# Stick-breaking heads with later ticks: running sums at tick 20, turned weights split at 38 and used at 41, gate turned at 8

## The chip, the cores and the metric

The kernel runs on one core of a Trainium2 chip. A core has TensorE (PE in the profile; its weight loads are listed apart, as PEld), VectorE (DVE), ScalarE (ACT), GpSimd (POOL) and SyncE (SP), which here only issues transfers. Each engine takes its instructions in the order in which the program issues them, and waits on semaphores for what the others make. The metric is the device time of one execution in microseconds (us), lower is better; the profile comes from one execution, recorded by the hardware profiler.

## What is computed

Two layers of a decoder trunk over 256 positions of width 2048, everything in float32, then a final RMSNorm. Layer 0 has sparse attention and dilated attention; layer 1 has eight stick-breaking heads (mixer C) and eight forgetting heads (mixer D). Each layer is a norm, one input projection whose columns are the heads' queries, keys, values and gates, the heads, a gate, and an output projection that is added to the stream. The change is in mixer C. For one block of 128 queries:

```python
z = jnp.einsum('bqhd,bshd->bhqs', qb, k).astype(F32) * (HEAD_DIM ** -0.5)
before = (key_pos[None, :] < qpos[:, None])[None, None]
log_1m = jnp.where(before, jax.nn.log_sigmoid(-z), 0.0)
tail = lax.cumsum(log_1m, axis=3, reverse=True) - log_1m
w = jnp.where(before, jnp.exp(jax.nn.log_sigmoid(z) + tail), 0.0)
return jnp.einsum('bhqs,bshd->bqhd', w.astype(v.dtype), v)
```

and behind the heads `x + (y * jax.nn.silu(gate)) @ w_out`. The kernel forms softplus(z) as relu(z) + log(1 + exp(-|z|)), sums it from the right with a scan, and takes the weight as exp(z - sum).

## The kernel before

**Chunks and k steps.** The columns of each input projection are cut into chunks, one per head: for a stick-breaking head 512 columns, queries, keys, values and gate of that head. Head 1 is the exception: its queries and keys stand in chunk F1 with the forget gates (264 columns), its values and gate in chunk G1 (256). `project` (line 328) multiplies a chunk in 16 k steps of 128 rows. In each step, for each half of the 256 positions, three matmuls are added in PSUM: high part of the activations by high part of the weights, low by high, and high by low (lines 323, 324, 326). So a k step of a full chunk is six matmuls of 512 columns.

**Splitting the weights.** A transfer brings four k steps of weights (1024 KB, tile `raw`, three buffers). `split` (line 267) makes the two parts of two k steps at a time, which I call a half: ScalarE copies to `whi` (line 282), VectorE subtracts to `wlo` (line 283), four buffers each. A chunk has eight halves, 0 to 7. Before the k steps of a half are issued, the halves up to three further on are split (line 360, `AHEAD`), so that the split of half 3 of a chunk is the first that is issued after the chunk has begun.

**Ticks.** The heads are Python generators. After each k step of a full chunk `tick` (line 307) advances a clock by one, and every generator whose count has run out goes on: it issues its next instructions on all engines, and with `yield n` stands back for n ticks. So the order of the work on every engine is written by hand, in ticks; 16 ticks make a full chunk, 8 each make F1 and G1. A head starts (its tick 0) when its own chunk has been projected, while the next chunk is multiplied. Where several generators are due at one tick, the one that was started first goes first.

**One stick-breaking head** (`head_c`, line 933; `head_cf` for head 1). Ticks are from its own start.

- 0: `scaled_qk` (line 840) scales queries and keys out of PSUM (ScalarE line 845, VectorE line 846), `grid` (line 420) turns their 32 x 32 blocks on VectorE (line 428), and `vg1` (line 849) makes values and gate: exponential (line 856), reciprocal (861), product (866), parts of the values (484, 487). This is the head's opening work.
- 2 and 6: the turned blocks of queries and keys are stored to DRAM and read back in another order, which completes the transposition (`moved`, line 431). Both transfers are issued by SP, which waits in order for each.
- 4, 6 and 10: the gate `u` goes the same way (`gate_turned`, line 494): blocks turned, stored, read into `uT`.
- 10: `qk_parts` (line 403) cuts queries and keys into parts (lines 408 to 410).
- 14: `scores` (line 514) on TensorE; VectorE adds the mask (line 915); ScalarE forms softplus and relu (lines 918 to 921).
- 16: VectorE makes the running sums (two scans, line 924) and the difference (line 926), ScalarE the exponential (line 927). Tick 16 falls at the end of the next head's chunk, just ahead of that head's tick 0.
- 18, 20 and 24: the weights `z` are turned in blocks (line 428), stored, and read back by four transfers (line 442).
- 28: `weights_out` (line 546) cuts the turned weights into parts `ph` and `pl` and a copy `p1`.
- 31: `weigh_out` (line 505) multiplies values by weights on TensorE (lines 461 to 463 and 510, tile `o`), VectorE multiplies by the gate (line 511), and the product is cut into its place for the output projection.

Head 0 reads its queries and keys at tick 8 and forms its values in three ticks, with the later stages at the same places. The forgetting heads (`head_d`) have the same opening work and a softmax in place of lines 915 to 927; their gate still goes by `gate_turned`.

**Buffers.** `z` shares two buffers with the softmax tiles, `uT` has two, `v` has two and a third place for heads 2, 5 and the first forgetting head; `ph`, `pl`, `p1` and `sp` have one each. `far`, into which `grid` turns, has two, and the DRAM tiles four.

Of the kernel before, what the change touches and what calls it, by code (L numbers as in the profile page):

```python
# [7 lines left out]
F32 = mybir.dt.float32  # L8
# [6 lines left out]
P = 128  # L15
NT = 2
SEQ = 256
# [157 lines left out]
def trunk(ctx, tc, x, xT, g1, w0, wo0, w1, wo1, bf, gf, consts, rope, out):  # L175
    nc = tc.nc
    cp = ctx.enter_context(tc.tile_pool(name="cp", bufs=1))
    wp = ctx.enter_context(tc.tile_pool(name="wp", bufs=3))
    hp = ctx.enter_context(tc.tile_pool(name="hp", bufs=2))
    dr = ctx.enter_context(tc.tile_pool(name="dr", bufs=1, space=bass.MemoryType.DRAM))  # L180
# [112 lines left out]
    def start(g):  # L293
        n = next(g, None)
        if n is not None:
            side.append([g, n])
# [116 lines left out]
    def quarters(a):  # L413
        return a.rearrange("p (b i c) -> p b i c", i=4, c=32)

    def arrived(t, n):

        return t.rearrange("p (i b c) -> p b i c", i=4, b=n)

    def grid(srcs):  # L420

        t = hp.tile([P, 512], F32, name="far", tag="rt2")
        ns = [x.shape[1] // P for x in srcs]
        n = sum(ns)
        o = t[:, 0:P * n].rearrange("p (j b c) -> p b j c", j=4, b=n)
        for i, x in enumerate(srcs):
            b = sum(ns[:i])
            nc.vector.transpose(o[:, b:b + ns[i]], x.rearrange("p (b j l) -> p b j l", j=4, l=32))  # L428
        return t[:, 0:P * n]

    def moved(t, dst, done, stored, ordered=False):


        n = t.shape[1] // P
        d = dr.tile([P, P * n], F32, name="fard", tag=f"fard{n}", bufs=4)
        yield done
        nc.sync.dma_start(d, t)
        yield stored
        if ordered:
            w = P * n // 4  # L440
            for j in range(4):
                nc.sync.dma_start(dst[32 * j:32 * j + 32].rearrange("p (i f) -> p i f", i=4),
                                  d[:, j * w:(j + 1) * w].rearrange("(i l) f -> l i f", i=4))
            return
        nc.sync.dma_start(dst.rearrange("p (i f) -> p i f", i=4),
                          d.rearrange("r (j f) -> (r j) f", j=4).rearrange("(i q) f -> q i f", i=4))

    def far(srcs, dst, first, done, stored):

        yield first  # L450
        yield from moved(grid(srcs), dst, done, stored)

    def qk_turned(qk, ticks, last):

        yield last or ticks
        r = qk_parts(quarters(turn([qk[:, i * P:(i + 1) * P] for i in range(4)])) if last else arrived(qk, 4))
        yield 6 - last if last else 4
        return qk_of(r)

    def three_of(o, ah, al, bh, bl, first, last):  # L460
        nc.tensor.matmul(o, ah, bh, start=first, stop=False)
        nc.tensor.matmul(o, ah, bl, start=False, stop=False)
        nc.tensor.matmul(o, al, bh, start=False, stop=last)
# [8 lines left out]
    def cut(dst, src):  # L472

        nc.scalar.activation(dst[0], src, AF.Copy)  # L474
        nc.vector.tensor_tensor(dst[1], src, dst[0].bitcast(F32), op=OP.subtract)  # L475
# [18 lines left out]
    def gate_turned(u, n=NT):  # L494
        uT = hp.tile([P, P * n], F32, name="uT", tag="uT" if n == NT else "rl")
        start(far([u], uT, 4, 2, 4))
        return arrived(uT, n)

    def gate_turned_here(u):
        pt = turn([u[:, 0:P], u[:, P:SEQ]])  # L500
        uT = hp.tile([P, SEQ], F32, name="uT", tag="uT")
        nc.scalar.activation(uT, pt[:, 0:SEQ], AF.Copy)
        return quarters(uT)

    def weigh_out(ph, pl, p1, v, uT, kt):

        vh, vl, v1 = v
        po = pa.tile([P, SEQ], F32, name="o", tag="o", bufs=1)
        three_of(po, vh, vl, ph, pl, True, False)
        nc.tensor.matmul(po[:, P:SEQ], v1, p1, start=False, stop=True)  # L510
        nc.vector.tensor_tensor(uT, quarters(po), uT, op=OP.mult)  # L511
        cut([quarters(t[:, kt, :]) for t in ys], uT)

    def scores(qk):
        q0, k0, q1h, q1l, kh, kl = qk
        pS = pa.tile([P, 384], F32, name="s", tag="s", bufs=1)
        nc.tensor.matmul(pS[:, 0:P], q0, k0, start=True, stop=True)  # L517
        three(pS[:, P:384], q1h, q1l, kh, kl)
        return pS
# [26 lines left out]
    def weights_out(blocks, v, uT, kt, last):  # L546

        ph = hp.tile([P, SEQ], F32R, name="ph", tag="ph", bufs=1)
        pl = hp.tile([P, SEQ], F32R, name="pl", tag="pl", bufs=1)
        p1 = hp.tile([P, P], F32, name="p1", tag="p1", bufs=1)  # L550
        cut((quarters(ph), quarters(pl)), blocks[:, 0:2])
        nc.scalar.activation(quarters(p1), blocks[:, 2:3], AF.Copy)
        if last:
            uT = gate_turned_here(u=uT)
        yield 2 if last else 3
        weigh_out(ph, pl, p1, v, uT, kt)

    def softmax_head(qk, ticks, nb, v, u, rs, kt, last, near):

        uT = u if last else gate_turned(u)  # L560
        qk = yield from qk_turned(qk, ticks, last)
        pr, l = soft(qk, nb() if callable(nb) else nb)
        if not last:
            yield 2
        share(pr, factor(l, rs))
        if near:
            yield 4
            blocks = quarters(turn([pr[:, 0:P], pr[:, P:SEQ], pr[:, SEQ:384]]))
        else:
            yield from moved(grid([pr]), pr, 2, 4, True)  # L570
            yield 4
            blocks = arrived(pr, 3)
        yield from weights_out(blocks, v, uT, kt, last)
# [165 lines left out]
    def heads_a(ps, h):  # L739
# [7 lines left out]
        for th in (1, 0):  # L747
            nc.vector.scalar_tensor_tensor(u[:, :, th, :], tgs[th].rearrange("p (a b) -> p a b", a=2), 1.0,
                                           ps[th][:, 256:512].rearrange("p (a b) -> p a b", a=2),
                                           op0=OP.add, op1=OP.mult)  # L750
        uT = gate_turned(u.rearrange("p a b c -> p (a b c)"), 4)
        yield from far([qk], qk, 2, 2, 4)
        yield 4
# [154 lines left out]

    def stick(qk, ticks, v, u, kt):

        uT = gate_turned(u)
        qk = yield from qk_turned(qk, ticks, 0)
        pZ = scores(qk)
        z = hp.tile([P, 384], F32, name="z", tag="sn")
        nc.vector.tensor_tensor(z, pZ, smask, op=OP.add)
        sp = hp.tile([P, 384], F32, name="sp", tag="sp", bufs=1)
        zp = hp.tile([P, 384], F32, name="zp", tag="ih", bufs=1)
        nc.scalar.activation(sp, z, AF.Abs)
        nc.scalar.activation(sp, sp, AF.Exp, scale=-1.0)
        nc.scalar.activation(sp, sp, AF.Ln, bias=1.0)  # L920
        nc.scalar.activation(zp, z, AF.Relu)
        yield 2
        for _, s in BLK:
            nc.vector.tensor_tensor_scan(sp[:, s][:, ::-1], sp[:, s][:, ::-1], zp[:, s][:, ::-1], 0.0,  # L924
                                         op0=OP.add, op1=OP.add)
        nc.vector.tensor_tensor(z, z, sp, op=OP.subtract)
        nc.scalar.activation(z, z, AF.Exp)
        yield 2
        yield from moved(grid([z]), z, 2, 4, True)
        yield 4  # L930
        yield from weights_out(arrived(z, 3), v, uT, kt, 0)

    def head_c(ps, h):
        qk = scaled_qk(ps, 0, (0, 3), (1, 2))
        start(moved(grid([qk]), qk, 2, 4))
        v, u = yield from vg1(ps, 256, h == 0, h % 3 == 2)
        yield from stick(qk, 10 if h else 8, v, u, h)

    def head_cf(ps, qk):
        v, u = yield from vg1(ps, 0)  # L940
        yield from stick(qk, 10, v, u, 1)
# [133 lines left out]
```

## Time and profile before

| | |
|---|---|
| median of 3 runs | 915.04 us (914.64 to 915.21) |
| the profiled execution | 914.97 us |
| its span, first to last instruction | 913.2 us |
| mean granted TensorE clock | 0.993 |
| PE busy | 888.4 us, 97% of the span |
| DVE busy | 656.5 us, 72% |
| ACT busy | 477.2 us, 52% |
| DMA | 203.65 MB, mean 223 GB/s |

The span is what lies between the first and the last instruction; the execution's time has 1.8 us more. Busy is the time in which an engine has an instruction at work; matmuls are pipelined, so that a busy PE need not be at its peak. The granted clock is the share of its full clock that TensorE was given. A row of the trace in order of time has start, duration, engine, line, operation, output<-inputs with their form, and, in brackets, how long the engine was idle before it and who released it. The stick-breaking heads lie between about 440 and 680 us of the span.

### The profile page before, as it was taken

To read this page: it belongs to the slowest core of one execution; us is meant where nothing else is said; L and a number is where in the kernel's file an instruction comes from. 1 tells how busy PE (TensorE), PEld (TensorE's weight loads), DVE (VectorE), ACT (ScalarE), POOL (GpSimd) and SP (SyncE) were. 2 spreads that over 40 slices of the span, in tenths; PEclk is the share of its full clock that TensorE was granted. 3 is DMA by queue.
4 is the path that set the end of the run, shared out by engine and by line. 5 is a ranking of instruction groups with operands and counts; after the bars stand their busy time and mean duration, and the time that the engine had idled before them with its cause. 6 is when DMAs were issued, how large, how long until landed. Compare 5 with 4: busy or idle time off the path is not lost.

```text
span 913.2 us, 11994 instructions
## 1 busy us (share of the span) xinstructions
PE 888.4 (97%) x4215; PEld 740.8 (81%) x4215; DVE 656.5 (72%) x1152; ACT 477.2 (52%) x840; POOL 49.5 (5%) x67
## 2 busy tenths in 40 slices
PE   9999999999999999999989999889999999999996
PEld 6988888888888888888978777777788888888886
DVE  7677889877777776666656767676677778876563
ACT  7654555555454555445464554555555555555450
POOL 0023000000000000000000000000000000001110
PEclk9999999999999999999999999999999999999999
DMA  9886656666565554666466665555676766665442
GB/s 359 328 313 233 231 191 224 227 238 233 205 220 193 205 206 174 248 248 235 150 238 225 237 228 176 193 178 193 230 274 242 265 242 242 236 217 184 184 184 93
DMA packets 82716, 203.65 MB, mean 223 GB/s; under 512 B 26192, under 2 KB 53600, under 8 KB 64736
## 3 DMA queue, kind: packets, MB, share of 16 engines
q1 hardware_dynamic: 81216, 199.58, 61.3%
q0 software_dynamic: 864, 2.12, 0.9%
q10 hardware_dynamic: 576, 1.19, 0.4%
q8 instruction: 33, 0.54, 0.2%
q14 instruction: 27, 0.22, 0.1%
HBM read 183.32 MB, written 19.54 MB: 222 GB/s over the span
## 4 chain that ended last, share of the span: by engine, by line
PE 77%; DVE 9%; ACT 4%; DMA 4%; issue 4%; SPq 1%; POOL 0%; DVEq 0%; POOLq 0%; ACTq 0%
PE pj L326 24%; PE pj L323 24%; PE pj L324 24%; DVE wlo L283 3%; ACT whi L282 2%; DVE e L861 2%; DMA qk<-fard 1%; DMA raw<-in_w_in_dram 1%; DMA z<-fard 1%; DVE far L428 1%; DVE sp L924 1%; PE s L517 1%; PE tp L400 1%; DVE qk L846 1%; DMA w0yh<-in_w_in_dram 1%
## 5 line engine op out<-in xcount | busy, mean ns | idle before, releaser
L283 DVE TENSOR_TENSOR wlo<-raw,whi 128x1024 fp32r<-128x1024 f32 (+3 forms) x300 | 352.0, 1191 | 134.7 <-ACT whi L282 133.2
L323 PE MATMUL pj<-whi,xh 128*128 128x512 f32 (+3 forms) x992 | 382.2, 387 | 3.0 <-ACT whi L282 2.9
L324 PE MATMUL pj<-whi,xl 128*128 128x512 f32 (+3 forms) x992 | 378.6, 383 | 0.0
L282 ACT ACTIVATE whi<-raw 128x1024 fp32r<-128x1024 f32 (+3 forms) x300 | 299.3, 1026 | 123.0 <-PE pj L324 99.7
L326 PE MATMUL pj<-wlo,xh 128*128 128x512 f32 (+3 forms) x992 | 300.2, 384 | 13.5 <-DVE wlo L283 13.4
L326 PEld LDWEIGHTS pj<-wlo,xh 128*128 128x128 f32 x992 | 184.3, 190 | 53.4 <-DVE wlo L283 18.2
L323 PEld LDWEIGHTS pj<-whi,xh 128*128 128x128 f32 x992 | 187.8, 189 | 39.7 <-ACT whi L282 6.8
L324 PEld LDWEIGHTS pj<-whi,xl 128*128 128x128 f32 x992 | 187.8, 189 | 32.8
L323 PE MATMUL pj<-whi,yh 128*128 128x512 f32 (+1 forms) x248 | 95.8, 386 | 0.0
L324 PE MATMUL pj<-whi,yl 128*128 128x512 f32 (+1 forms) x248 | 95.0, 383 | 0.0
L326 PE MATMUL pj<-wlo,yh 128*128 128x512 f32 (+1 forms) x248 | 76.7, 383 | 0.0
L326 PEld LDWEIGHTS pj<-wlo,yh 128*128 128x128 f32 x248 | 46.6, 188 | 9.2
L323 PEld LDWEIGHTS pj<-whi,yh 128*128 128x128 f32 x248 | 46.7, 188 | 8.7
L324 PEld LDWEIGHTS pj<-whi,yl 128*128 128x128 f32 x248 | 46.7, 188 | 8.7
L530 ACT ACTIVATE sn<-sn,nm 128x128 f32<-128x128 f32 (+1 forms) x48 | 21.5, 449 | 42.2 <-DVE nm L528 42.2
L474 ACT ACTIVATE yh<-uT 128x256 fp32r<-128x256 f32 (+1 forms) x27 | 12.4, 457 | 49.1 <-DVE uT L511 38.7
L577 ACT ACTIVATE sq<-xs 128x512 f32<-128x512 f32 x23 | 14.3, 623 | 28.7 <-DVE xs L800 26.9
L861 DVE RECIPROCAL e<-e 128x256 f32<-128x256 f32 x16 | 28.0, 1753 | 0.5
L408 ACT ACTIVATE qkh<-qk 128x384 fp32r<-128x384 f32 x20 | 10.3, 517 | 30.7 <-DMA qk<-fard 30.7
L382 POOL TENSOR_TENSOR qk<-rot,rot 128x256 f32<-128x256 f32 x16 | 11.8, 739 | 229.4 <-ACT sn L530 111.0
L410 DVE TENSOR_TENSOR qkl<-qk,qkh 128x384 fp32r<-128x384 f32 x20 | 11.1, 557 | 17.8 <-ACT qkh L408 17.7
L475 DVE TENSOR_TENSOR yl<-uT,yh 128x256 fp32r<-128x256 f32 (+1 forms) x27 | 12.8, 475 | 14.3 <-ACT yh L474 14.3
(216 smaller groups left out, 711.5 us busy)
## 6 DMA issues: line engine op xcount, KB each, us to landing
raw<-in_w_in_dram SPq DMA_DIRECT2D x108, 1024.0 KB, 6.2
raw<-in_w_out_dram SPq DMA_DIRECT2D x32, 1024.0 KB, 4.9
fard<-far SPq DMA_DIRECT2D x43, 256.0 KB, 2.1
qk<-fard SPq DMA_DIRECT2D x25, 256.0 KB, 4.5
fard<-far SPq DMA_DIRECT2D x18, 192.0 KB, 1.8
raw<-in_w_in_dram SPq DMA_DIRECT2D x4, 672.0 KB, 9.8
fard<-far SPq DMA_DIRECT2D x20, 128.0 KB, 4.9
uT<-fard SPq DMA_DIRECT2D x20, 128.0 KB, 4.8
```

The lines of the kernel that those rows point to most:

```text
L282: nc.scalar.activation(hi, rw, AF.Copy)
L283: nc.vector.tensor_tensor(lo, rw, hi.bitcast(F32), op=OP.subtract)
L323: nc.tensor.matmul(o, a, wh, start=(kt == 0), stop=False)
L324: nc.tensor.matmul(o, b, wh, start=False, stop=False)
L326: nc.tensor.matmul(o, a, wl, start=False, stop=(kt == KT - 1))
L382: nc.gpsimd.tensor_tensor(dst, t1[:, 0:n], t2[:, 0:n], op=OP.add)
L410: nc.vector.tensor_tensor(quarters(lo), blocks[:, 1:4], quarters(hi).bitcast(F32), op=OP.subtract)
L474: nc.scalar.activation(dst[0], src, AF.Copy)
L475: nc.vector.tensor_tensor(dst[1], src, dst[0].bitcast(F32), op=OP.subtract)
L530: nc.scalar.activation(sn[:, s], sn[:, s], AF.Exp, scale=-1.0, bias=nm[:, th:th + 1], accum_out=l[:, th:th + 1])
L577: nc.scalar.activation(j, xs[:, th, c * 512:(c + 1) * 512], AF.Square, accum_out=ss[:, i, th, c:c + 1])
L861: nc.vector.reciprocal(e, e)
```

## The change

Three places in `stick`, and what they call. The running sums wait six ticks behind the scores instead of two, so they come at tick 20; blocks of `z` are turned at 22, stored at 24 and read at 28. The wait between that read and the cut grows from four ticks to ten: `weights_out` cuts at 38, and `weigh_out` multiplies at 41, in the chunk after next. The gate gets a function of its own, `gate_late`: its blocks are turned at tick 8 instead of 4, stored at 10, read at 14, and the tile `uT` is taken only at the read, where `gate_turned` takes it at tick 0. It hands over a list that holds `uT` by the time that `weigh_out` asks for it. The last lines of `moved` become a function, `read_back`, with the same transfer.

```diff
-        nc.sync.dma_start(dst.rearrange("p (i f) -> p i f", i=4),
-                          d.rearrange("r (j f) -> (r j) f", j=4).rearrange("(i q) f -> q i f", i=4))
+        read_back(dst, d, n)
+
+    def read_back(dst, d, n):
+        nc.sync.dma_start(dst.rearrange("p (i f) -> p i f", i=4),
+                          d.rearrange("r (j f) -> (r j) f", j=4).rearrange("(i q) f -> q i f", i=4))
...
+    def gate_late(u):
+        box = []
+        def way():
+            yield 8
+            t = grid([u])
+            d = dr.tile([P, SEQ], F32, name="fard", tag="fard2", bufs=4)
+            yield 2
+            nc.sync.dma_start(d, t)
+            yield 4
+            uT = hp.tile([P, SEQ], F32, name="uT", tag="uT")
+            read_back(uT, d, NT)
+            box.append(arrived(uT, NT))
+        start(way())
+        return box
...
-        weigh_out(ph, pl, p1, v, uT, kt)
+        weigh_out(ph, pl, p1, v, uT[0] if isinstance(uT, list) else uT, kt)
...
     def stick(qk, ticks, v, u, kt):
-        uT = gate_turned(u)
+        uT = gate_late(u)
         qk = yield from qk_turned(qk, ticks, 0)
         pZ = scores(qk)
...
-        yield 2
+        yield 6
         for _, s in BLK:
             nc.vector.tensor_tensor_scan(sp[:, s][:, ::-1], sp[:, s][:, ::-1], zp[:, s][:, ::-1], 0.0,
                                          op0=OP.add, op1=OP.add)
...
         yield 2
         yield from moved(grid([z]), z, 2, 4, True)
-        yield 4
+        yield 10
         yield from weights_out(arrived(z, 3), v, uT, kt, 0)
```

## The prediction, made before the changed kernel was run

> **What bounds the kernel now.** I read the page first, then who waited for whom on TensorE, then the busy time of each stretch of the stage with the stick-breaking heads, then the order of time at one boundary between two chunks there.
>
> ```profile
> span 913.2 us, 11994 instructions
> ...
> PE 888.4 (97%) x4215; PEld 740.8 (81%) x4215; DVE 656.5 (72%) x1152; ACT 477.2 (52%) x840; POOL 49.5 (5%) x67
> ```
>
> The profiled execution took 914.97 us, 1.8 of them outside the span, and stands 0.07 below the median, 915.04. TensorE is the bound, with 24.8 us idle in all. The waits say where 16.3 of them lie:
>
> ```profile
> PE pj L326 <- DVE wlo L283: 13.4, 8, 1.8
> PE pj L323 <- ACT whi L282: 2.9, 5, 1.0
> ```
>
> These are waits for the split of the weights into a high part (whi, ScalarE) and a low part (wlo, VectorE). Eight for wlo, and there are eight stick-breaking heads. The stretches (columns: span, busy time and count of PE, weight load, VectorE, ScalarE, GpSimd, then granted clock, DMA share, GB/s) put them at chunk boundaries and nowhere else:
>
> ```profile
> 470.00:480.00 10.00, 7.68 (x30) 5.41 (x31) 8.35 (x13) 6.37 (x11) 0.00 (x0) 1.00 0.31 105
> 480.00:485.00 5.00, 5.00 (x19) 4.01 (x18) 4.85 (x6) 1.78 (x3) 0.00 (x0) 0.66 0.77 258
> ...
> 503.00:508.00 5.00, 3.46 (x16) 2.53 (x15) 4.96 (x7) 3.47 (x4) 0.00 (x0) 1.00 0.15 57
> ...
> 529.00:536.00 7.00, 5.17 (x15) 3.86 (x15) 6.96 (x10) 3.87 (x5) 0.00 (x0) 0.76 0.42 134
> ...
> 556.00:561.00 5.00, 3.46 (x16) 2.53 (x15) 4.96 (x9) 3.15 (x4) 0.00 (x0) 1.00 0.24 66
> ...
> 580.00:587.00 7.00, 4.32 (x18) 2.91 (x17) 6.93 (x11) 5.12 (x9) 0.00 (x0) 1.00 0.23 76
> ...
> 606.00:614.00 8.00, 5.29 (x16) 3.65 (x16) 7.90 (x13) 4.87 (x9) 0.00 (x0) 0.79 0.28 85
> ...
> 634.00:639.00 5.00, 3.46 (x16) 2.55 (x15) 4.96 (x8) 3.15 (x5) 0.00 (x0) 1.00 0.23 87
> ...
> 658.00:665.00 7.00, 5.02 (x21) 3.49 (x21) 6.93 (x11) 5.15 (x9) 0.00 (x0) 1.00 0.18 68
> 665.00:705.00 40.00, 40.00 (x187) 33.30 (x186) 30.55 (x56) 20.67 (x43) 1.98 (x3) 1.00 0.81 282
> ```
>
> In each of these VectorE is busy nearly throughout. Idle of PE: 2.32 + 1.54 + 1.83 + 1.54 + 2.68 + 2.71 + 1.54 + 1.98 = 16.1 us. Three times the granted clock falls behind the stall: 0.34 × 5, 0.24 × 7 and 0.21 × 8 us are lost, 1.7 each, 5.1 together. The last row is the forgetting heads: no idle, although VectorE works as much. One boundary, VectorE alone:
>
> ```profile
> 574.42 1.23 DVE L283 TENSOR_TENSOR wlo<-raw,whi 128x1024 fp32r<-128x1024 f32 x1 [3.07 <-ACT whi L282]
> ...
> 576.81 1.00 DVE L924 TENSOR_TENSOR_SCAN sp<-sp,zp 128x128 f32<-128x128 f32 x2
> 577.84 0.56 DVE L926 TENSOR_TENSOR z<-z,sp 128x384 f32<-128x384 f32 x1
> 579.25 0.61 DVE L846 TENSOR_SCALAR qk<-pj,rstd 128x128 f32<-128x128 f32 x2 [0.85 <-ACT qk L845]
> ...
> 580.88 1.75 DVE L861 RECIPROCAL e<-e 128x256 f32<-128x256 f32 x1
> ...
> 583.45 1.22 DVE L283 TENSOR_TENSOR wlo<-raw,whi 128x1024 fp32r<-128x1024 f32 x1
> 584.58 0.58 DVE L428 STREAM_TRANSPOSE far<-z 128x384 f32<-128x384 f32 x1
> ```
>
> The head's running sums (tick 16) meet the next head's opening work (tick 0), and between them no weights are split: 9.0 us from one wlo to the next, where PE uses one up every two k steps. PE at the same place, and its pace:
>
> ```profile
> 572.51 0.40 PE L323 MATMUL pj<-whi,xh 128*128 128x512 f32 x1
> ...
> 576.61 0.39 PE L323 MATMUL pj<-whi,xh 128*128 128x512 f32 x1
> ...
> 582.57 0.40 PE L324 MATMUL pj<-whi,xl 128*128 128x512 f32 x1
> 584.73 0.74 PE L326 MATMUL pj<-wlo,xh 128*128 128x512 f32 x2 [1.76 <-DVE wlo L283]
> ```
>
> Three k steps from 572.51 to 576.61: 1.36 us each, which is a tick. I call 572.51 T, the start of the chunk on PE. It needs the late wlo (half 3 of eight) six ticks and four matmuls later, about T+9.1, and gets it at 584.67. From 582.57 to 584.73 are 2.16 us, less one matmul's 0.23 it is 1.93, so a stall costs 0.17 more than its idle.
>
> **Removed.** Scans, subtraction and exponential leave the boundary for tick 20, which is tick 4 of the next chunk. What then stands between two wlo is the opening work alone: 579.25 to 583.45, 4.2 us. The boundary of a forgetting head has that and more, and no idle:
>
> ```profile
> 769.51 1.23 DVE L283 TENSOR_TENSOR wlo<-raw,whi 128x1024 fp32r<-128x1024 f32 x1 [1.66 <-ACT whi L282]
> 770.65 0.16 DVE L536 RECIPROCAL sc<-l 128x2 f32<-128x2 f32 x1
> ...
> 776.10 2.35 DVE L283 TENSOR_TENSOR wlo<-raw,whi 128x1024 fp32r<-128x1024 f32 x2
> ```
>
> One of the thirteen waits is no boundary's, and stays:
>
> ```profile
> 470.13 0.50 PE L323 MATMUL pj<-whi,xh 128*128 128x512 f32 x1 [0.44 <-ACT whi L282]
> ```
>
> Worth: idle 16.1 − 0.44, the restart of the other twelve, 12 × 0.17, and the clock's 5.1, which I count with the stalls since each slow stretch starts behind one and the stage has no other: 22.8 us.
>
> "TensorE: Matmul & The Clock Gate" of the Trainium skill (Part 1) has the clock halve only after an idle window of about 3.4 us. No idle here is over 2.7, yet the clock falls behind three of eight stalls; by that rule the slow stretches would have another cause and stay, and the sum would be 17.7.
>
> **Moved, and what is late next.** The weights' cut goes from tick 28 to 38 and their product from 31 to 41: ticks 6 and 9 of the chunk after next, behind the moved scans. I walk one chunk with these rows:
>
> ```profile
> 571.39 0.53 ACT L918 ACTIVATE sp<-z 128x384 f32<-128x384 f32 x1 [1.76 <-DVE z L915]
> ...
> 573.35 1.04 ACT L282 ACTIVATE whi<-raw 128x1024 fp32r<-128x1024 f32 x1
> ...
> 578.44 0.52 ACT L927 ACTIVATE z<-z 128x384 f32<-128x384 f32 x1 [2.00 <-DVE z L926]
> 578.87 0.61 ACT L845 ACTIVATE qk<-pj,rr 128x128 f32<-128x128 f32 x2
> ...
> 580.65 3.91 ACT L282 ACTIVATE whi<-raw 128x1024 fp32r<-128x1024 f32 x4
> ```
>
> ```profile
> L408 ACT ACTIVATE qkh<-qk 128x384 fp32r<-128x384 f32 x8 | 4.2, 523 | 28.0 <-DMA qk<-fard 28.0
> ...
> L475 DVE TENSOR_TENSOR pl<-z,ph 128x256 fp32r<-128x256 f32 x8 | 3.4, 420 | 0.0
> ...
> L474 ACT ACTIVATE ph<-z 128x256 fp32r<-128x256 f32 x8 | 3.2, 406 | 1.1 <-DMA z<-fard 1.1
> ```
>
> Now ScalarE's L918 stands at T−1.1. I take it 0.7 earlier, since two DMA waits ahead of it (28.0 us on qk, 1.1 on z) go: the read of qk no longer stands behind the store of z on SP's queue, and z has ten ticks to arrive instead of four. Then the whi of half 2 ends at T+1.2, its wlo at T+2.35, the opening work at T+6.55, two wlo (the row of 776.10, 2.35) at T+8.9. The first is there at T+7.7 against T+9.1: no stall at the boundary. Scans to T+9.9 (576.81 to 577.84), difference to T+10.5 (to 578.44), exponential to T+10.9 (to 578.87). ScalarE stands at the exponential for all that time, and behind it in its queue is the whi of half 5: it comes only then, 1.04, to T+11.95; its wlo, 1.2, to T+13.1, in time for PE, which wants it five halves and four matmuls on, at T+14.5. Behind that whi is ph (0.41: T+12.4), behind that wlo is pl (0.42: T+13.5). PE reaches the product at tick 9, T+12.3, and its second matmul needs pl: it waits 1.1 us, and every projection matmul stands behind it.
>
> The walk adds whole durations, while rows in succession overlap (four whi in 3.91 are 0.98 each, not 1.04; 846 starts before the second 845 ends); I take 0.75 of waiting and 0.15 of restart, 0.9. Seven chunks have both a scan at tick 4 and a product at tick 9 (heads 0 to 6), so 6.3 us. Head 7's product falls where no scan is: nothing. Bounds: no wait, if ScalarE comes 1.1 earlier than walked; 1.8 + 0.15, if L918 stays at T−1.1.
>
> By Part 2 of the same page matmuls stay in program order and only weight loads are pulled ahead; the stall at 584.73 agrees, with the next step's whi ready (ScalarE's row of four). Were it otherwise this wait would be free, and the time that of the first rival.
>
> **The rest at nothing.** Gate: the same transpose, store and read four ticks later (8, 10, 14), where VectorE is past its opening work; the read is wanted 27 ticks (37 us) on. If that cover were gone, each tick that it came late would be 1.36 us of the multiplication behind the product, on VectorE, not on PE. SP's queue: store of z at tick 8, store of u at 10, four reads of z at 12; the loads of weights behind them wait for a wlo each anyway, and three buffers of four k steps lie ahead. No instruction is added. The longer lives of z, v and uT cost nothing: every tile is free again before its slot's next use (the slot of v is used every third head; uT is now taken at tick 14).
>
> Sum: 914.97 − 22.8 + 6.3 = 898.5 us.
>
> **Rivals.**
>
> - No new wait: 914.97 − 22.8 = 892.2. For it: the walk's 1.1 us are little against the 1.76 that ScalarE now waits ahead of L918. Against: VectorE is close to full.
> - A long new wait, 1.95 a head, and the clock falls behind three of eight as now: 7 × 1.95 + 7 × 3/8 × 1.7 = 18.1, so 910.3; without the clock 905.8. For it: the old T−1.1.
> - The clock falls here for a reason of its own and the slow stretches stay: 898.5 + 5.1 = 903.6. For it: five stalls of the eight have none, one of 2.68 among them. Against: all three start right behind a stall.
> - Slower: VectorE reaches the scans 2.2 us later than walked, half of the 4.4 by which the wlo now stands at T+10.9 instead of T+6.55. Then pl comes 3.3 late (7 × 3.45 = 24.2), half 3's wlo 0.8 late at eight boundaries (8 × 0.97 = 7.8), and the clock's 5.1 stay: 914.97 − 22.8 + 37.1 = 929. It decides from a wait of 22.8 / 7 = 3.3 us. Against: nothing in the walk is that long.
> - The boundary's stall is only moved to the scans' new place, whole: 915. Against: the boundary at 770.
>
> **How the numbers follow.** Chances: forecast 0.44, no new wait 0.21, long wait 0.12, slow stretches 0.10, slower 0.08, moved whole 0.05. The forecast's own range, with waits of 0.5 to 1.4, is 895.6 to 901.9. Over all I take 890 to 909: 2 us below the no-wait case, since the restart of a stall is sized by one row, and up to just short of the long wait with its slow clock. A measurement here tells about 0.2% from no change. Faster 0.85 (all of the first four but the long wait's tail), same 0.05, slower 0.10.
>
> **What would show it.** Right: the eight waits of L326 for wlo gone; instead PE waits at the matmul L462 of tile o for pl, seven times, under 1.4 us; clock 1.00 through the stage; the exponential L927 waits about 5 us per head for its difference; qkh no longer waits for its DMA. Wrong: wlo waits at the boundaries again, waits for pl over 2 us, or a raw tile's DMA as releaser.

## The result and the profile after

The changed kernel takes 898.62 us (median of 4 runs, 897.81 to 900.5), the kernel before on the same chip 914.84 (914.19 to 915.21): a ratio of 0.9826, 95% interval 0.9809 to 0.9843. The forecast was 898.5 us. The profiled executions stand at 898.54 and 914.97 us.

The page of the kernel after, its span and TensorE's share:

```profile
span 896.8 us, 12002 instructions
...
PE 881.5 (98%) x4215; PEld 738.2 (82%) x4215; DVE 656.2 (73%) x1152; ACT 475.1 (53%) x840; POOL 49.2 (5%) x67
```

The span is 16.4 us shorter with the same work on every engine. TensorE's idle fell from 24.8 to 15.3 us, 9.5 of the 16.4; most of the rest is its clock, of which the profile before lost 5.1 us and this one nothing in the stage with the stick-breaking heads. That stage in one row (columns: stretch, its length, busy time and count of PE, weight load, VectorE, ScalarE, GpSimd, granted clock, DMA share, GB/s), first before, then after:

```profile
475.00:690.00 215.00, 199.08 (x881) 161.24 (x880) 152.88 (x230) 113.36 (x199) 4.01 (x6) 0.98 0.60 211
```

```profile
475.00:690.00 215.00, 208.66 (x956) 172.15 (x956) 163.38 (x252) 119.54 (x216) 4.73 (x7) 1.00 0.68 231
```

In the same 215 us TensorE idles 6.3 instead of 15.9 and has its full clock throughout. Those 6.3 us are one kind of wait, by the list of who waited for whom on TensorE (total us, times, longest):

```profile
PE o L465 <- DVE pl L478: 6.3, 7, 0.9
```

Line 465 is the matmul that was line 462 (the functions have moved down), in the product of values and turned weights; line 478 was 475. The eight waits for wlo and the five for whi are gone. One chunk in order of time, TensorE first, whose first row is the start of the chunk (T = 563.29):

```profile
563.29 0.39 PE L323 MATMUL pj<-whi,xh 128*128 128x512 f32 x1
...
575.52 0.31 PE L464 MATMUL o<-ph,v 128*128 128x256 f32 x1
576.74 0.39 PE L465 MATMUL o<-pl,v 128*128 128x256 f32 x1 [0.91 <-DVE pl L478]
576.96 0.28 PE L466 MATMUL o<-ph,v 128*128 128x256 f32 x1
577.08 0.38 PE L531 MATMUL o<-p,v 128*128 128x128 f32 x2
577.22 0.47 PE L323 MATMUL pj<-whi,xh 128*128 128x512 f32 x1
577.53 0.39 PE L324 MATMUL pj<-whi,xl 128*128 128x512 f32 x1
```

The product's first matmul runs, the second waits for pl. From 575.52 to 576.74 are 1.22 us where two such matmuls follow each other at 0.12 otherwise: 1.1 us lost, 0.91 of them idle. The matmuls behind them come a little late too: from 575.52 to 577.53 are 2.01 us, and 0.81 at the same place in a kernel without this wait (570.79 to 571.60, shown below with the exponential at 21). So a wait costs 1.2 us. VectorE and ScalarE at the same place:

```profile
564.38 1.23 DVE L283 TENSOR_TENSOR wlo<-raw,whi 128x1024 fp32r<-128x1024 f32 x1 [3.07 <-ACT whi L282]
565.53 0.60 DVE L867 TENSOR_SCALAR qk<-pj,rstd 128x128 f32<-128x128 f32 x2
...
569.73 2.35 DVE L283 TENSOR_TENSOR wlo<-raw,whi 128x1024 fp32r<-128x1024 f32 x2
571.99 1.00 DVE L945 TENSOR_TENSOR_SCAN sp<-sp,zp 128x128 f32<-128x128 f32 x2
573.03 0.56 DVE L947 TENSOR_TENSOR z<-z,sp 128x384 f32<-128x384 f32 x1
575.13 1.23 DVE L283 TENSOR_TENSOR wlo<-raw,whi 128x1024 fp32r<-128x1024 f32 x1 [1.54 <-ACT whi L282]
576.27 0.42 DVE L478 TENSOR_TENSOR pl<-z,ph 128x256 fp32r<-128x256 f32 x1
```

```profile
561.35 0.53 ACT L939 ACTIVATE sp<-z 128x384 f32<-128x384 f32 x1 [2.36 <-DVE z L936]
...
563.31 1.04 ACT L282 ACTIVATE whi<-raw 128x1024 fp32r<-128x1024 f32 x1
...
573.62 0.53 ACT L948 ACTIVATE z<-z 128x384 f32<-128x384 f32 x1 [4.68 <-DVE z L947]
574.05 1.04 ACT L282 ACTIVATE whi<-raw 128x1024 fp32r<-128x1024 f32 x1
575.00 0.40 ACT L477 ACTIVATE ph<-z 128x256 fp32r<-128x256 f32 x1
```

Between two wlo at the boundary now stand 5.35 us (564.38 to 569.73) instead of 9.0. The scans follow two wlo later, at tick 4. ScalarE waits 4.68 us at the exponential; behind it come the whi of half 5 and ph, and VectorE, idle for 1.54 us, can only then make the wlo and pl.

### The profile page after: what moved, and what is told of

Its sections match the earlier page's. It is cut to its first block, busy times and chain, and to the rows that moved or that the text cites. A ratio compares the mean times of both kernels' runs of the same rounds, so it can differ in the third digit from the quotient of the medians.

```text
span 896.8 us, 12002 instructions
## 1 busy us (share of the span) xinstructions
PE 881.5 (98%) x4215; PEld 738.2 (82%) x4215; DVE 656.2 (73%) x1152; ACT 475.1 (53%) x840; POOL 49.2 (5%) x67
## 4 chain that ended last, share of the span: by engine, by line
PE 75%; DVE 9%; DMA 7%; ACT 4%; issue 3%; SPq 1%; POOL 0%; POOLq 0%; DVEq 0%; ACTq 0%
PE pj L323 23%; PE pj L326 23%; PE pj L324 23%; DMA qk<-fard 4%; DVE wlo L283 3%; DMA raw<-in_w_in_dram 2%; ACT whi L282 2%; DVE e L882 1%; DVE far L428 1%; PE s L538 1%; PE tp L400 1%; DMA w0yh<-in_w_in_dram 1%; PE o L465 1%; DVE qk L867 0%; PE s L466 0%
## 5 line engine op out<-in xcount | busy, mean ns | idle before, releaser
L326 PE MATMUL pj<-wlo,xh 128*128 128x512 f32 (+3 forms) x992 | 296.6, 380 | 0.1
L948 ACT ACTIVATE z<-z 128x384 f32<-128x384 f32 x8 | 4.2, 526 | 38.0 <-DVE z L947 38.0
L877 ACT ACTIVATE e<-pj,nr 128x128 f32<-128x128 f32 x32 | 11.8, 368 | 21.6 <-DVE qk L867 21.6
```

The lines of the kernel that those rows point to most:

```text
L326: nc.tensor.matmul(o, a, wl, start=False, stop=(kt == KT - 1))
L877: nc.scalar.activation(e[:, t], ps[th][:, o + P:o + 256], AF.Exp, scale=nr1[:, th:th + 1])
```

## The experiments

The theory: the boundary's loss came from the running sums standing in front of the next head's opening work, and the new wait comes from ScalarE's exponential, behind which the split of half 5 and then pl queue up. The main rival: VectorE is simply full in these chunks, and a wait that is removed returns elsewhere. The four kernels of a group were timed on one chip, together with the kernel before.

| kernel | us, median | ratio to the kernel before, 95% interval |
|---|---|---|
| the change | 898.62 | 0.9826 (0.9809 to 0.9843) |
| sums at 20 alone | 892.94 | 0.9767 (0.9738 to 0.9796) |
| late end alone | 903.27 | 0.9878 (0.9854 to 0.9901) |
| the change, product at 42 | 894.32 | 0.9782 (0.9760 to 0.9803) |
| the change, exponential at 21 | 889.45 | 0.9725 (0.9703 to 0.9746) |
| the change, old gate | 899.03 | 0.9846 (0.9817 to 0.9876) |
| the change, cut at 36 | 895.32 | 0.9807 (0.9778 to 0.9836) |
| before, exponential at 17 | 902.47 | 0.9885 (0.9859 to 0.9911) |
| sums at 20, exponential at 21 alone | 891.22 | 0.9756 (0.9730 to 0.9783) |

The kernel before had a median of 914.84 us beside the first row, 914.88 beside the second to fifth, and 913.19 beside the others.

**The sums alone.** Against the change:

```diff
-        uT = gate_late(u)
+        uT = gate_turned(u)
...
-        yield 10
+        yield 4
         yield from weights_out(arrived(z, 3), v, uT, kt, 0)
```

> Only the running sums move to tick 20; gate by the old function, and four ticks between the read of the turned weights and their cut, so the cut is at tick 32 and the product at 35. If the boundary's idle comes from the sums standing in front of the opening work, it goes here as in the change. The cut is now issued ahead of the opening work and the sums, so the product at tick 35 should not wait for pl, and the seven waits of 0.91 us (1.1 with restart, 7.7 in all) should be missing: 891 us; if the product's gate work (about 1.3 us on VectorE) delays the sums so far that the split of half 5 comes late, up to 0.3 us a chunk more: 893. Rival (the late cut and use carry part of the gain, since they clear the boundary too): waits for wlo come back at the boundaries, 0.5 to 1 us each, 899 to 903.

It took 892.94 us. TensorE's waits:

```profile
PE pj L323 <- ACT whi L282: 1.5, 3, 0.8
...
PE pj L326 <- DVE wlo L283: 0.8, 1, 0.8
PE o L464 <- ACT ph L477: 0.4, 1, 0.4
```

All boundaries but the last are clear (the wait for wlo is at 663.84) and no product waits for pl, so the move of the sums, by itself, is worth more than the whole change (0.9767 against 0.9826): some 5 us of its gain are lost again by the rest of it. The rival, by which the boundary needs the late end too, fails. The move takes ScalarE's exponential off the boundary together with VectorE's sums; this run does not tell the two apart.

**The end alone.** Against the change:

```diff
         nc.scalar.activation(zp, z, AF.Relu)
-        yield 6
+        yield 2
...
-        yield 10
+        yield 14
         yield from weights_out(arrived(z, 3), v, uT, kt, 0)
```

> Only the end moves: running sums at tick 16 as before, cut of the turned weights at 38, product at 41, gate at 8. What leaves the boundary is the product's gate work of tick 31 (1.3 us on VectorE between two wlo). Theory: the sums are the larger part, so waits for wlo stay at eight boundaries, shorter, 0.5 to 1.0 us each instead of 1.5 to 2.7, and the clock may or may not fall behind them: 900 to 906. Rival (the sums alone matter): 914 to 915. Second rival (only the end matters): 892 to 899.

```profile
PE pj L326 <- DVE wlo L283: 9.1, 8, 1.8
PE pj L323 <- ACT whi L282: 2.2, 3, 1.2
```

903.27 us, inside what was expected: all eight waits for wlo stay, now 9.1 us instead of 13.4. Moving the product's gate work away from the boundary helps there too: before, it stands between a wlo and the sums (575.56 to 576.81), and here the sums follow the wlo at once. But the boundary keeps its sums. The waits for wlo and whi make 5.0 of the 11.7 us between the two profiled executions, and 5.1 are the clock, which is 1.00 in this stage here. The late gate is part of this run; at the old sums it was not tried by itself.

**The product one tick later.** Against the change, in `weights_out`:

```diff
-        yield 2 if last else 3
+        yield 2 if last else 4 if isinstance(uT, list) else 3
```

> The change with the product one tick later, at 42. pl is there 0.91 us after PE wants it at tick 41, and a tick is 1.36 us: the seven waits at the product go, nothing else moves: 898.6 - 7 x 1.1 = 890.9 us. Rival (VectorE is too full in these chunks, and a wait removed at one place returns as a late wlo further on): waits for wlo or whi appear in ticks 10 to 16, 895 to 899.

894.32 us: a gain of 4.3 us, about half of what the theory gave, and near the rival's range, though no wait comes up where the rival had it (ticks 10 to 16). TensorE still waits at the product; the list, and three of the six in order of time:

```profile
PE o L465 <- DVE pl L478: 3.1, 6, 0.8
```

```profile
551.03 0.38 PE L465 MATMUL o<-pl,v 128*128 128x256 f32 x1 [0.50 <-DVE pl L478]
...
574.77 0.38 PE L465 MATMUL o<-pl,v 128*128 128x256 f32 x1 [0.51 <-DVE pl L478]
...
598.51 0.39 PE L465 MATMUL o<-pl,v 128*128 128x256 f32 x1 [0.51 <-DVE pl L478]
```

The waits are 23.74 us apart. After the change VectorE waits for TensorE's scores at tick 14 in most chunks (1.6 us in five of them between 500 and 640 us); here it waits for them in none of that stretch. So it is VectorE and ScalarE, taking turns, that set the pace: they need 23.74 us for a chunk. With the wait at tick 41 TensorE gave them time (24.16 us from one product to the next, 504.25 to 528.41 in the profile after the change), and that hid it.

**The exponential one tick later.** Against the change:

```diff
         nc.vector.tensor_tensor(z, z, sp, op=OP.subtract)
+        yield 1
         nc.scalar.activation(z, z, AF.Exp)
-        yield 2
+        yield 1
         yield from moved(grid([z]), z, 2, 4, True)
```

> The change with the exponential of the weights one tick behind the difference, at tick 21 instead of 20; product still at 41. Theory: pl is late because ScalarE stands at the exponential and the split of half 5, and behind it pl, queue up; with the exponential one tick later ScalarE splits half 5 first (about 4 us earlier), VectorE goes from the difference straight to that wlo (it now idles 1.5 us there), and pl comes about 1 us earlier: the seven waits go or shrink to 0.2 us: 891 to 893 us. Rival (VectorE itself is full up to there, whatever ScalarE does): the waits stay at 0.7 to 0.9 us, 897 to 899.

889.45 us, the fastest of all, 25 us below the kernel before, and below the 891 to 893 that were expected: the expectation took 1.1 us a wait, and seven at 1.2 are 8.4 of the 9.2 us that went. VectorE and ScalarE at one chunk, TensorE at the product, and the stage in one row:

```profile
567.26 1.00 DVE L945 TENSOR_TENSOR_SCAN sp<-sp,zp 128x128 f32<-128x128 f32 x2
568.29 0.56 DVE L947 TENSOR_TENSOR z<-z,sp 128x384 f32<-128x384 f32 x1
568.77 1.22 DVE L283 TENSOR_TENSOR wlo<-raw,whi 128x1024 fp32r<-128x1024 f32 x1
569.90 0.42 DVE L478 TENSOR_TENSOR pl<-z,ph 128x256 fp32r<-128x256 f32 x1
```

```profile
568.88 0.53 ACT L949 ACTIVATE z<-z 128x384 f32<-128x384 f32 x1 [3.73 <-DVE z L947]
...
591.85 0.53 ACT L949 ACTIVATE z<-z 128x384 f32<-128x384 f32 x1 [3.73 <-DVE z L947]
```

```profile
570.79 0.28 PE L464 MATMUL o<-ph,v 128*128 128x256 f32 x1
...
571.60 0.40 PE L324 MATMUL pj<-whi,xl 128*128 128x512 f32 x1
```

```profile
475.00:690.00 215.00, 215.00 (x994) 179.34 (x993) 169.92 (x261) 122.37 (x222) 6.00 (x9) 1.00 0.71 241
```

VectorE goes from the difference to the wlo with no idle: the 1.54 us are gone. A chunk takes 22.97 us (568.88 to 591.85), 1.2 less than with the wait, and TensorE has no idle left in the stage. This shows the cause of the product's wait: not the work on VectorE, which is the same, but its standing still for a ScalarE that stands still for it.

**The cut ahead of the sums.** Against the change, cut at tick 36, product still at 41:

```diff
-        yield 2 if last else 3
+        yield 2 if last else 5 if isinstance(uT, list) else 3
...
-        yield 10
+        yield 8
         yield from weights_out(arrived(z, 3), v, uT, kt, 0)
```

> The change with the cut of the turned weights at tick 36 instead of 38, product still at 41. The cut is then issued ahead of the next head's sums and exponential, so PE finds pl at tick 9; but the exponential still stands in front of the split of half 5, and VectorE still idles 1.5 us for it. Theory from the product at 42 (VectorE and ScalarE together need 23.74 us for a chunk there, PE 22.97): the product's waits go, but the two fall behind by 0.77 us a chunk, and after two chunks PE waits for wlo instead: 893 to 896. Rival (the product's wait was the whole loss): no waits of PE at all, 889 to 891.

```profile
PE pj L326 <- DVE wlo L283: 3.0, 6, 0.8
PE pj L323 <- ACT whi L282: 1.8, 2, 1.4
```

```profile
572.00 0.73 PE L326 MATMUL pj<-wlo,xh 128*128 128x512 f32 x2 [0.46 <-DVE wlo L283]
...
595.74 0.74 PE L326 MATMUL pj<-wlo,xh 128*128 128x512 f32 x2 [0.45 <-DVE wlo L283]
```

895.32 us, as the theory had it. pl is in time, and the waits are back at wlo, six of them, the two shown again 23.74 us apart: the same pace of the two engines, seen at another place. So the main rival is half right: while ScalarE's exponential stands in the way, a wait that is removed does return.

**The old gate.** Against the change:

```diff
-        uT = gate_late(u)
+        uT = gate_turned(u)
```

> The change with the gate's old function: its blocks turned at tick 4, store at 6, read at 10; the rest as changed. Theory (the gate part is worth nothing by itself): at tick 4 the transpose of the gate, 0.36 us, falls into the 1.5 us in which VectorE idles for the split of half 5, so pl is as late as before, 7 x 0.91: 898 to 899.5 us. Rival (VectorE is the bound there and the gate had to go): pl 0.36 us later in seven chunks, 901 to 902.

899.03 us, the same as the change. VectorE at the sums:

```profile
573.82 0.56 DVE L947 TENSOR_TENSOR z<-z,sp 128x384 f32<-128x384 f32 x1
574.29 0.44 DVE L428 STREAM_TRANSPOSE far<-u 128x256 f32<-128x256 f32 x1
575.92 1.23 DVE L283 TENSOR_TENSOR wlo<-raw,whi 128x1024 fp32r<-128x1024 f32 x1 [1.18 <-ACT whi L282]
```

The gate's transpose fits into the idle time before the wlo, which shrinks from 1.54 to 1.18 us; pl is as late as before.

**The exponential at 17 in the kernel before.** The sums stay at the boundary:

```diff
         nc.vector.tensor_tensor(z, z, sp, op=OP.subtract)
+        yield 1
         nc.scalar.activation(z, z, AF.Exp)
-        yield 2
+        yield 1
         yield from moved(grid([z]), z, 2, 4, True)
```

> The kernel before with one thing changed: the exponential at tick 17 instead of 16, behind the next head's opening work and the split of half 3. VectorE's sums stay at the boundary. Theory: ScalarE no longer waits 2.0 us for the difference ahead of its opening work, VectorE saves the 0.85 us in which it waits for ScalarE's queries, so each of the eight boundaries is about 0.85 us shorter: 907 to 909 us, with waits for wlo left at all boundaries. Rival (only the sums on VectorE matter): 914 to 915. Rival (ScalarE's waiting exponential is the main cause at the boundary too): under 900.

902.47 us, below what either the theory (907 to 909) or the first rival gave, and above the second rival's 900. TensorE's waits, and VectorE at a boundary:

```profile
PE pj L326 <- DVE wlo L283: 9.8, 9, 1.7
```

```profile
569.68 0.56 DVE L926 TENSOR_TENSOR z<-z,sp 128x384 f32<-128x384 f32 x1
570.16 0.60 DVE L846 TENSOR_SCALAR qk<-pj,rstd 128x128 f32<-128x128 f32 x2
...
574.35 1.22 DVE L283 TENSOR_TENSOR wlo<-raw,whi 128x1024 fp32r<-128x1024 f32 x1
```

VectorE goes from the difference to the opening work in 0.48 us, where the kernel before took 1.41 (577.84 to 579.25), and TensorE's waits for its weights fall from 16.3 to 9.8 us: 6.5, or 0.81 a boundary where 0.85 was expected. Left out of the expectation was the clock, of which the profile of the kernel before lost 5.1 us in this stage, and this one nothing (row below). Of the 13.1 us between the two profiled executions the waits and the clock make 11.6. That the clock explains the miss of the median is not shown: two runs of this kernel, at a mean clock of 0.996 and of 0.999, took 901.98 and 901.91 us.

```profile
475.00:690.00 215.00, 205.50 (x940) 168.34 (x939) 158.29 (x247) 115.53 (x210) 4.71 (x7) 1.00 0.66 229
```

**The sums at 20 and the exponential at 21, nothing else.** Against the change, the old gate, `yield 4` before the cut, and the exponential one tick behind the difference.

> Sums at tick 20, exponential at 21, everything else at the old distances: cut at 32, product at 35, old gate function. If the late end and the late gate are not needed, this is as fast as the change with the exponential at 21 (889.5), at most 2 us slower where the last stick-breaking head meets the first forgetting heads (2.0 us were lost there with the sums alone): 889 to 892. Rival (the late end is needed to clear ticks 0 to 3): waits return at boundaries, over 893.

```profile
475.00:690.00 215.00, 214.98 (x993) 179.00 (x992) 167.64 (x259) 121.77 (x217) 5.99 (x9) 1.00 0.69 240
```

891.22 us (889.35 to 891.73); the interval overlaps that of the 889.45. No idle in the stage, at the old distances of cut, product and gate. The late end and the late gate are not needed.

## Why the prediction was right, and where its terms were off

- *What bounds the kernel* held. The boundary's waits went with the sums, and all but the last went when the sums alone were moved. How much of this is ScalarE's exponential, which moves with them, the prediction did not ask; by itself, one tick later in the kernel before, it was worth 11 us.
- *The walk* held nearly to the tenth. On its scale, with T = 563.29: ScalarE's softplus at T−1.9 (walked −1.8), half 2's wlo done at T+2.3 (2.35), opening work done at T+6.4 (6.55), sums begun at T+8.7 (8.9), exponential left at T+10.8 (10.9), product reached at T+12.2 (12.3), pl done at T+13.4 (13.5). Seven waits for pl, as counted. ScalarE's waits for the DMA of qk, 28.0 us before in this stage, are gone, as the walk's earlier start assumed.
- *The size of the new wait* is a term that was mis-sized. The walk gave 1.1 us a chunk and I cut it to 0.9 for overlaps. It measured 1.2 (0.91 of idle, the rest restart): 8.4 us, not 6.3.
- *The size of the old stalls* was too small by as much. 16.4 us less span and 8.4 of new waits make 24.8 us removed, where I had 22.8. One part is the restart: I took 0.17 us from the late matmul alone, and those behind it are late too. In the profile before:

```profile
573.21 0.39 PE L324 MATMUL pj<-whi,xl 128*128 128x512 f32 x1
...
573.89 0.39 PE L323 MATMUL pj<-whi,xh 128*128 128x512 f32 x1
...
582.57 0.40 PE L324 MATMUL pj<-whi,xl 128*128 128x512 f32 x1
...
585.31 0.40 PE L323 MATMUL pj<-whi,xh 128*128 128x512 f32 x1
```

The stall makes 2.74 us out of 0.68, so 2.06 for 1.76 of idle: a restart of 0.30, and for twelve stalls, by this one row, 1.6 us more. The other part is the wait at 470 us (0.4), which I said stays: it is not in the profile after. It is in that of the sums alone (one of its three waits for whi), so its absence is not shown to be the change's doing. These two make up the 2.0, but not to better than a microsecond: the profile after also has a wait of 0.6 us ahead of the stage (at 210.86) that the one before lacks. The two errors of 2.1 and 2.0 us cancel by luck, and the forecast is closer than its terms.
- *The slow stretches* went with the stalls, as the sum had it: the clock is 1.00 in the stage, and the mean clock of the four runs 0.997 to 0.999. The rival by which they have a cause of their own and stay (903.6 us) does not hold here. The rule behind it is that of "TensorE: Matmul & The Clock Gate" of the Trainium skill (Part 1), that the clock halves after an idle window of about 3.4 us. The profile before has it fall behind stretches with 1.8 to 2.7 us of idle.
- *The first rival* had a wrong price. I gave 892.2 us for a product that finds pl in time. The cut at 36 does just that and takes 895.3, since VectorE and ScalarE need 23.74 us for a chunk. I had put "VectorE is close to full" beside it as an objection and not carried it to a number; and fullness was not the cause: with the exponential at 21 VectorE does the same work in 22.97 us a chunk.
- *The gate at nothing* held: 899.03 against 898.62.
- *A part I had as needed cost something.* I costed the late cut and product as one move with the sums. Alone the sums gave 892.9; the late end added the wait for pl.

## What to carry to other kernels

On engines that work through their instructions in order, an instruction that waits for another engine costs what is queued behind it, so look at what stands behind a long wait before asking whether the engines are full: here one exponential, moved by one tick, was worth 9 us after the change and 11 before it (there not by its wait alone, as said above). When a wait is moved, walk the queue at the new place with the durations of the trace; that gave the new wait to about a tenth of a microsecond, and the cut made for overlaps took it further off. And price the move's parts one by one: the part that is only meant to make room may be the one that costs.

## What the runs showed of the hardware

The granted clock falls behind waits of TensorE that are well under 3 us, and not each time. In the first profile of the kernel before it fell behind three of eight boundaries, at the stretches that begin at 470, 529 and 606 us (idle 2.3, 1.8 and 2.7), each time for a loss of 1.7 us, and not in the one at 580 (idle 2.7). In 14 runs of that kernel the mean granted clock lay between 0.990 and 0.998, and the times between 916.1 us (at 0.990) and 910.4 (at 0.994; 911.4 and 911.5 at 0.998 and 0.997): the clock explains at most a part of that spread. With the exponential at 17 in that kernel, runs at 0.996 and 0.999 took the same 902 us. With the late end alone, waits of up to 1.8 us left the mean clock of the profiled run at 0.999. What decides whether it falls was not tried.
